# Hybrid attention encoder layer on one Trainium2 core: last down product in one group of nine feature pairs, sum over heads as two adds

## The chip, the cores and the metric

The kernel runs on one core of one Trainium2 chip. The metric is device time in microseconds (us); the figure for a kernel is the median of its runs. All tensors are float32. A matmul operand is split into a rounded high part and a remainder, and a product is made of three matmuls: high by high, high by remainder and remainder by high.

## The reference, cut to what matters

One encoder layer over 2048 tokens of width 1024. Half of the heads attend to all tokens, half to a window; each half is normalised over its 512 columns, and the two go through one output projection. A gated feed-forward block with 2816 features follows.

```python
def rms_norm(x, g):
    y = x * lax.rsqrt(jnp.mean(x * x, axis=-1, keepdims=True) + EPS)
    return y * g

mixed = jnp.concatenate([rms_norm(out_a, group_norm_a), rms_norm(out_b, group_norm_b)], -1) @ w_out
x = x + rms_norm(mixed, norm_mix_post)
h = rms_norm(x, norm_ffn_pre)
f = (jax.nn.silu(h @ w_gate) * (h @ w_up)) @ w_down
x = x + rms_norm(f, norm_ffn_post)
```

## The kernel before, in words

The program runs in stages: input projection and windowed attention (to about 590 us), the global attention with the output projection woven in (to about 1230 us), a short passage to the feed-forward part, the gate and up products, and the down products, which end the program. TensorE is PE below, VectorE DVE, ScalarE ACT, GpSimd POOL, and SP the engine that issues the DMAs.

**The planner.** Nearly all instructions are first recorded and then ordered by a planner (class `Plan`, from line 257). It has a cost for each instruction and latencies between engines, orders the whole program up to four times and keeps the pass that it finds shortest. Each engine executes its own queue strictly in the planned order, so an instruction that waits holds up all that stand behind it on its engine. As every instruction is issued from one place, the profile gives line 523 for all of them, and the rows are told apart by their tiles. A second copy of the program for large scores stands behind a branch and isn't executed.

**The sum over heads.** `out_half` (line 1418) handles one half (512 columns, 4 groups of 128) of one of the 16 token tiles, so it is called 32 times. It splits the half into `oh` and `ol`, squares it on ACT into the tile `sqo` (one buffer), and adds the four groups on DVE into `rd`, 128 x 128, at line 1445. A tiny matmul with `ones` sums `rd` further, and from this the scale `rg` of the half is made, with which the projected half leaves the PSUM.

```python
sq = op.tile([P, 512], F32, tag="sqo", bufs=1, name="sqo")
nc.scalar.activation(sq, o, AF.Square)
rd = op.tile([P, P], F32, tag="rd", bufs=1, name="rd")
nc.vector.tensor_reduce(rd, sq.rearrange("p (h c) -> p c h", h=4), axis=AX.X, op=ALU.add)
```

**The down products.** The feed-forward matrices are multiplied by a scheme of seven products of sums of quarters instead of eight. Each down product `p` is done for two halves `c` of the tokens. It adds over 11 feature pairs `j` (`NJ`) into four accumulators, one for each of four token tiles. For a pair it needs the activation side (`a_combo`, line 1683: a 256 KB load into `ar`, `ah` on ACT, `al` on DVE; four slots of each) and the weight side (`wd_combo`: `wdh` and `wdl`, 16 slots of each, 13 in one pool and 3 in another; a weight is kept for both values of `c`). `down_product` (line 1693) goes through the pairs in groups; within a group it takes accumulator by accumulator. Groups are single pairs, except in the very last call (`p` = 2, `c` = 1), whose last group has `TAIL` = 3 pairs.

**The end.** After the last product each of its four token tiles is finished (`finish`, line 1769): DVE adds the accumulator to a running total (tile `C`), ACT squares it (`junkf`) with a running sum, DVE multiplies by the gain (`gfp`) and adds the sums of squares (`fs`), POOL takes the power -1/2 (`fr`), and DVE, or for the second half of a row ACT and POOL, scale and add the residual (`st`), which SP writes out. For the last tile both halves are done on DVE. The residual rows are loaded into `st`, from `X`; of these buffers there are four.

Of the kernel before, what the change touches and what calls it, by code (L numbers as in the profile page):

```python
# [11 lines left out]
F32R = mybir.dt.float32r  # L12
AF = mybir.ActivationFunctionType
ALU = mybir.AluOpType
AX = mybir.AxisListType
# [3 lines left out]
P = 128  # L19
# [7 lines left out]
CH = 512  # L27
# [42 lines left out]
W_BUFS = 4  # L70
WD_L = 13
WD_R = 3
TAIL = 3
B_DVE = 13
B_DVE_U = (0, 2)
T_HI = 1
# [9 lines left out]
def f32(ap):  # L86
    return ap.bitcast(F32)
# [438 lines left out]
class Layer:  # L526
# [107 lines left out]
    def bank(self, pool, tag, bufs=1):  # L634
        return pool.tile([P, 512], F32, tag=tag, bufs=bufs, name=tag)
# [782 lines left out]
    def out_half(self, t, j, bank=None):  # L1418

        nc, op, sm = self.nc, self.op, self.sm  # L1420
        bank = bank or (lambda: self.bank(self.ps_a, "ow"))
        if j:
            o = op.tile([P, 512], F32, tag="ob", bufs=1, name="ob")
            self.load(o, self.OB[t])
            self.mixed[t] = op.tile([P, D], F32, tag="mix", bufs=1, name="mix")
        else:
            o = self.fin.pop(t)
        mix_ = self.mixed[t]
        h_ = op.tile([P, 512], F32R, tag="oh", name="oh")
        l_ = op.tile([P, 512], F32R, tag="ol", name="ol")  # L1430
        w = P if t == NT - 1 and j == 0 else 512
        for c in range(0, 512, w):
            self.urgent(LAST_UP if w == P else 0.0)
            nc.vector.tensor_copy(h_[:, c:c + w], o[:, c:c + w])
            self.urgent(0.0)
            yield GAP
            self.urgent(LAST_UP if w == P else 0.0)
            nc.vector.tensor_tensor(l_[:, c:c + w], o[:, c:c + w], f32(h_[:, c:c + w]), op=ALU.subtract)
            self.urgent(0.0)
            yield GAP  # L1440
        sq = op.tile([P, 512], F32, tag="sqo", bufs=1, name="sqo")
        nc.scalar.activation(sq, o, AF.Square)
        yield GAP
        rd = op.tile([P, P], F32, tag="rd", bufs=1, name="rd")
        nc.vector.tensor_reduce(rd, sq.rearrange("p (h c) -> p c h", h=4), axis=AX.X, op=ALU.add)
        rg = sm.tile([P, 1], F32, tag="rg", name="rg")

        def norm():
            self.urgent(HALF_UP if t == NT - 1 else 0.0)
            gs = bank()  # L1450
            nc.tensor.matmul(gs[:, 0:2], lhsT=rd, rhs=self.ones2, start=True, stop=True)
            self.rsqrt(rg, gs[:, 0:1], 512, 1)
            self.urgent(0.0)

        late = w == P
        if not late:
            norm()
            yield 430
        acc = [bank() for n in range(2)] if late else []
        for n in range(2):  # L1460
            cs = slice(n * 512, (n + 1) * 512)
            ps = acc[n] if late else bank()
            for p in range(4):
                pc = slice(p * P, (p + 1) * P)
                k = 4 * j + p
                nc.tensor.matmul(ps, lhsT=h_[:, pc], rhs=self.wo[2 * n][:, k], start=(p == 0), stop=False)
                yield 216
                nc.tensor.matmul(ps, lhsT=h_[:, pc], rhs=self.wo[2 * n + 1][:, k], start=False, stop=False)
                yield 216
                nc.tensor.matmul(ps, lhsT=l_[:, pc], rhs=self.wo[2 * n][:, k], start=False, stop=(p == 3))  # L1470
                yield 216
            if late and n == 0:
                norm()
            yield GAP2
            self.urgent(HALF_UP if t == NT - 1 else 0.0)
            if j:
                nc.scalar.activation(mix_[:, cs], ps, AF.Copy, scale=rg)
            else:
                nc.vector.scalar_tensor_tensor(mix_[:, cs], ps, rg, mix_[:, cs], op0=ALU.mult, op1=ALU.add)
            self.urgent(0.0)  # L1480
            yield GAP
        if not j:
            self.load(self.MX[t], self.mixed.pop(t))
# [174 lines left out]
    def wd_combo(self, p, j):  # L1658

        nc, fd = self.nc, self.fd  # L1660
        if p in self.B_SRC:
            src = self.wd_quarter(j, *self.B_SRC[p])
        elif p == 5:
            src = self.T[j] = self.fr.tile([P, CH], F32, tag=f"T{j}", bufs=1, name=f"T{j}")
            nc.gpsimd.tensor_tensor(src, self.wd_quarter(j, 0, 1), self.wd_quarter(j, 0, 0), op=ALU.subtract)
        elif p == 6:
            src = self.T[j]
            nc.gpsimd.tensor_tensor(src, self.wd_quarter(j, 1, 1), src, op=ALU.subtract)
        elif p == 4:
            src = self.T[j]  # L1670
            nc.gpsimd.tensor_tensor(src, src, self.wd_quarter(j, 1, 0), op=ALU.subtract)
        else:
            src, b = self.wd_quarter(j, 1, 1), self.wd_quarter(j, 0, 1)
            nc.gpsimd.tensor_tensor(src, src, b, op=ALU.subtract)
        pool, n = (fd, WD_L) if self.nwd % (WD_L + WD_R) < WD_L else (self.fr, WD_R)
        self.nwd += 1
        wh = pool.tile([P, CH], F32R, tag="wdh", bufs=n, name="wdh")
        wl = pool.tile([P, CH], F32R, tag="wdl", bufs=n, name="wdl")
        nc.scalar.activation(wh, src, AF.Copy)
        nc.vector.tensor_tensor(wl, src, f32(wh), op=ALU.subtract)  # L1680
        return wh, wl

    def a_combo(self, p, c, j):
        nc, fd = self.nc, self.fd
        st = fd.tile([P, CH], F32, tag="ar", bufs=3, name="ar")
        self.load(st, self.AC[c][j][:, p - 1])
        ah = fd.tile([P, CH], F32R, tag="ah", bufs=4, name="ah")
        al = fd.tile([P, CH], F32R, tag="al", bufs=4, name="al")
        nc.scalar.activation(ah, st, AF.Copy)
        nc.vector.tensor_tensor(al, st, f32(ah), op=ALU.subtract)  # L1690
        return ah, al

    def down_product(self, p, c, W, last=False):
        nc = self.nc
        acc = [self.gu_bank() for _ in range(4)]
        ends = list(range(1, self.NJ - TAIL + 1)) + [self.NJ] if last else range(1, self.NJ + 1)
        j0 = 0
        for j1 in ends:
            ops = []
            for j in range(j0, j1):  # L1700
                if (p, j) not in W:
                    W[p, j] = self.wd_combo(p, j)
                ops.append((j, *self.a_combo(p, c, j), *W[p, j]))
            for i in range(4):
                ts = slice(i * P, (i + 1) * P)
                for j, ah, al, wh, wl in ops:
                    nc.tensor.matmul(acc[i], lhsT=ah[:, ts], rhs=wh, start=(j == 0), stop=False)
                    nc.tensor.matmul(acc[i], lhsT=ah[:, ts], rhs=wl, start=False, stop=False)
                    nc.tensor.matmul(acc[i], lhsT=al[:, ts], rhs=wh, start=False, stop=(j == self.NJ - 1))
            j0 = j1  # L1710
        return acc
# [121 lines left out]
```

## Time and profile before

| | |
|---|---|
| median of 3 runs | 2554.9 us (2551.17 to 2563.43) |
| the profiled execution | 2557.14 us, its span 2555.3 us |
| busy in the span: PE, PE weight load | 2462.4 us (96%), 1945.0 us (76%) |
| busy in the span: DVE, ACT, POOL | 1877.8 us (73%), 1393.1 us (55%), 1473.4 us (58%) |

The span runs from the first to the last instruction in the profile; the rest of the execution's time lies around it. A row of a group shows its instructions' busy time, count and mean duration, then the idle time of its engine just before them and what ended it. A row of the timeline shows start, duration, engine and instruction; several alike in a row stand as x2, x3, with the time from the first start to the last end.

### The profile page before, as it was taken

The numbers are of one execution on the slowest core, as the hardware profiler recorded it, in microseconds if no ns is written. First come the engines' busy times: TensorE is split into PE (matmuls) and PEld (weight loads), VectorE is DVE, ScalarE is ACT, GpSimd is POOL, SyncE is SP. The second block draws the span as 40 slices with busy tenths as digits, with TensorE's granted clock in tenths as the row PEclk, the third lists the DMA queues.
The fourth block names the chain that finished last, engine by engine and source line by source line (L and its number), as shares of the span: only waits on it lengthen the run. The fifth ranks groups of instructions, "written<-read, shape, count | busy, mean of one in ns | idle before, by whom it ended". The sixth has DMA issues, their size and how long they took to land.

```text
span 2555.3 us, 34171 instructions
## 1 busy us (share of the span) xinstructions
PE 2462.4 (96%) x10604; PEld 1945.0 (76%) x10604; DVE 1877.8 (73%) x2864; ACT 1393.1 (55%) x2610; POOL 1473.4 (58%) x1175
## 2 busy tenths in 40 slices
PE   8999999899999999999899999999999999999997
PEld 6766677577877777777688888878888887888886
DVE  6777677789898988888877667796655556556755
ACT  5666566598888888878433333343332334433433
POOL 4333343379998889999365666755445443331333
PEclk9999999999999999999999999999999999999999
DMA  6555544443121313222544445563233227554664
GB/s 200 153 157 158 159 146 129 144 157 100 61 88 64 100 63 107 96 91 92 173 147 142 159 154 166 179 223 112 91 97 122 87 83 262 174 182 148 184 200 154
DMA packets 200896, 351.67 MB, mean 138 GB/s; under 512 B 26624, under 2 KB 82304, under 8 KB 200192
## 3 DMA queue, kind: packets, MB, share of 16 engines
q1 hardware_dynamic: 200704, 349.40, 42.5%
q8 instruction: 85, 1.39, 0.2%
q14 instruction: 107, 0.88, 0.1%
HBM read 229.85 MB, written 106.56 MB: 132 GB/s over the span
## 4 chain that ended last, share of the span: by engine, by line
PE 75%; DVE 7%; ACT 6%; DMA 5%; issue 4%; POOL 2%; SPq 1%; ACTq 0%; DVEq 0%; POOLq 0%
PE gu L523 31%; PE gv L523 18%; PE mm L523 6%; PE ow L523 6%; PE o L523 6%; PE a L523 4%; PE pp L523 3%; DVE pla L523 1%; DMA xn<-in_x_dram 1%; SPq L523 1%; ACT pha L523 1%; ACT mm L523 1%; POOL acc L523 1%; ACT nat L523 1%; DMA RB<-HL 1%
## 5 line engine op out<-in xcount | busy, mean ns | idle before, releaser
L523 POOL TENSOR_TENSOR acc<-acc,pha 128x512 f32<-128x512 f32 x408 | 561.3, 1386 | 48.9 <-ACT pha L523 22.5
L523 POOL TENSOR_TENSOR s<-wraw 128x512 f32<-128x512 f32 x88 | 124.3, 1425 | 304.4 <-DMA wraw<-in_w_up_dram 179.5
L523 PE MATMUL gu<-xl,wh 128*128 128x512 f32 x776 | 294.1, 396 | 0.0
L523 PE MATMUL gu<-xh,wl 128*128 128x512 f32 x776 | 288.1, 397 | 4.2 <-DVE wl L523 4.1
L523 PE MATMUL gu<-xh,wh 128*128 128x512 f32 x776 | 288.2, 397 | 1.8 <-ACT wh L523 1.8
L523 DVE TENSOR_TENSOR pla<-mm,pha 128x512 fp32r<-128x512 f32 x370 | 246.3, 682 | 34.4 <-ACT pha L523 24.0
L523 ACT ACTIVATE wh<-s 128x512 fp32r<-128x512 f32 x176 | 110.8, 630 | 281.5 <-PE gu L523 160.4
L523 PE MATMUL mm<-R,kt 128*128 128x512 f32 x740 | 251.0, 400 | 6.0 <-DVE pla L523 4.9
L523 PE MATMUL pp<-w_in,xh 128*128 128x512 f32 x720 | 239.2, 404 | 16.5 <-ACT w_in L523 10.9
L523 POOL TENSOR_TENSOR c<-c,c 128x512 f32<-128x512 f32 x132 | 203.4, 1557 | 77.5 <-DVE c L523 52.3
L523 DVE TENSOR_TENSOR al<-ar,ah 128x512 fp32r<-128x512 f32 x154 | 140.1, 913 | 146.9 <-ACT ah L523 131.7
L523 ACT ACTIVATE mm<-mm 128x512 f32<-128x512 f32 x370 | 214.6, 591 | 28.5 <-PE mm L523 26.1
L523 ACT ACTIVATE ah<-ar 128x512 fp32r<-128x512 f32 x154 | 97.0, 630 | 224.7 <-PE gu L523 137.2
L523 DVE TENSOR_TENSOR c<-gu,c 128x512 f32<-128x512 f32 x174 | 116.4, 686 | 115.8 <-PE gu L523 115.3
L523 DVE TENSOR_TENSOR wl<-s,wh 128x512 fp32r<-128x512 f32 x176 | 164.9, 942 | 20.9 <-ACT wh L523 11.5
L523 PE MATMUL gv<-xl,wh 128*128 128x512 f32 x456 | 175.1, 396 | 2.2 <-DVE xl L523 2.2
L523 PEld LDWEIGHTS gu<-xh,wl 128*128 128x128 f32 x776 | 146.1, 189 | 39.2 <-DVE wl L523 5.0
L523 ACT ACTIVATE wh<-wraw 128x512 fp32r<-128x512 f32 x132 | 83.0, 628 | 168.3 <-PE gu L523 97.6
L523 PEld LDWEIGHTS gu<-xh,wh 128*128 128x128 f32 x776 | 146.3, 189 | 36.9 <-ACT wh L523 2.7
L523 PEld LDWEIGHTS mm<-R,kt 128*128 128x128 f32 x740 | 134.7, 188 | 50.2 <-DVE pla L523 21.2
L523 PEld LDWEIGHTS pp<-w_in,xh 128*128 128x128 f32 x720 | 136.0, 191 | 48.5 <-ACT w_in L523 13.1
L523 PEld LDWEIGHTS gu<-xl,wh 128*128 128x128 f32 x776 | 146.4, 189 | 34.5
(257 smaller groups left out, 6522.0 us busy)
## 6 DMA issues: line engine op xcount, KB each, us to landing
AC<-c SPq DMA_DIRECT2D x154, 256.0 KB
ar<-AC SPq DMA_DIRECT2D x154, 256.0 KB
wdr<-in_w_down_dram SPq DMA_DIRECT2D x99, 256.0 KB
wraw<-in_w_gate_dram SPq DMA_DIRECT2D x20, 1024.0 KB
wraw<-in_w_up_dram SPq DMA_DIRECT2D x20, 1024.0 KB
R<-QA SPq DMA_DIRECT2D x128, 128.0 KB
st<-XB SPq DMA_DIRECT2D x40, 256.0 KB
xn<-in_x_dram SPq DMA_DIRECT2D x16, 512.0 KB
```

Of the source, the lines that this page charges most:

```text
L523: op.call(*[real(a) for a in op.args], **{k: real(v) for k, v in op.kw.items()})
```

## The change

Two edits. `TAIL` goes from 3 to 9, so the last call's groups are pair 0, pair 1, and then pairs 2 to 10 together. Nine pairs need nine slots for the activation side at once, where there are four; the activation sides of pairs 2 to 6 go into weight slots of which five are free by then (16 less the 11 weights of that product), through the new argument `spare`. In the planned order these five read `wdh<-ar` and `wdl<-ar`. In `out_half` the reduction becomes two additions, 128 x 256 in place in `sqo` and 128 x 128 into `rd`.

```diff
-TAIL = 3
+TAIL = 9
...
-        nc.vector.tensor_reduce(rd, sq.rearrange("p (h c) -> p c h", h=4), axis=AX.X, op=ALU.add)
+        nc.vector.tensor_tensor(sq[:, 0:2 * P], sq[:, 0:2 * P], sq[:, 2 * P:4 * P], op=ALU.add)
+        nc.vector.tensor_tensor(rd, sq[:, 0:P], sq[:, P:2 * P], op=ALU.add)
...
+        wh, wl = self.wd_tiles()
...
-    def a_combo(self, p, c, j):
+    def wd_tiles(self):
+        pool, n = (self.fd, WD_L) if self.nwd % (WD_L + WD_R) < WD_L else (self.fr, WD_R)
+        self.nwd += 1
+        return [pool.tile([P, CH], F32R, tag=tag, bufs=n, name=tag) for tag in ("wdh", "wdl")]
+
+    def a_combo(self, p, c, j, spare=False):
         nc, fd = self.nc, self.fd
         st = fd.tile([P, CH], F32, tag="ar", bufs=3, name="ar")
         self.load(st, self.AC[c][j][:, p - 1])
-        ah = fd.tile([P, CH], F32R, tag="ah", bufs=4, name="ah")
-        al = fd.tile([P, CH], F32R, tag="al", bufs=4, name="al")
+        if spare:
+            ah, al = self.wd_tiles()
+        else:
+            ah = fd.tile([P, CH], F32R, tag="ah", bufs=4, name="ah")
+            al = fd.tile([P, CH], F32R, tag="al", bufs=4, name="al")
...
-                ops.append((j, *self.a_combo(p, c, j), *W[p, j]))
+                ops.append((j, *self.a_combo(p, c, j, last and j < j1 - 4 and j >= self.NJ - TAIL), *W[p, j]))
```

Since the planner orders the program as a whole, its order differs from the first use of `rd` on, about 590 us into the program, and not only where instructions were exchanged.

The end of DVE's queue, the work on the last token tiles (`C` a running total, `fs` a sum of squares, `st` an output row). Before:

```order
L523 TENSOR_TENSOR C_21369<-gu,C_21369 128x512
L523 SCALAR_TENSOR_TENSOR fs_24439<-fsq 128x1
L523 TENSOR_TENSOR C_21369<-C_21369,gfp 128x512
L523 SCALAR_TENSOR_TENSOR fs_24451<-fsq 128x1
L523 TENSOR_TENSOR C_21369<-C_21369,gfp 128x512
L523 TENSOR_TENSOR C_21369<-gu,C_21369 128x512
L523 SCALAR_TENSOR_TENSOR st<-C_21369,fr,st 128x512
L523 TENSOR_TENSOR C_21369<-C_21369,gfp 128x512
L523 SCALAR_TENSOR_TENSOR fs_24465<-fsq 128x1
L523 SCALAR_TENSOR_TENSOR st<-C_21369,fr,st 128x512
L523 SCALAR_TENSOR_TENSOR st<-C_22428,fr,st 128x512
L523 SCALAR_TENSOR_TENSOR st<-C_21369,fr,st 128x512
```

and now:

```order
L523 SCALAR_TENSOR_TENSOR fs_24449<-fsq 128x1
L523 TENSOR_TENSOR C_21384<-C_21384,gfp 128x512
L523 SCALAR_TENSOR_TENSOR st<-C_21384,fr,st 128x512
L523 TENSOR_TENSOR C_21384<-gu,C_21384 128x512
L523 SCALAR_TENSOR_TENSOR fs_24483<-fsq 128x1
L523 TENSOR_TENSOR C_21384<-C_21384,gfp 128x512
L523 SCALAR_TENSOR_TENSOR st<-C_21384,fr,st 128x512
L523 TENSOR_TENSOR C_21384<-gu,C_21384 128x512
L523 TENSOR_TENSOR C_21384<-C_21384,gfp 128x512
L523 SCALAR_TENSOR_TENSOR fs_24501<-fsq 128x1
L523 SCALAR_TENSOR_TENSOR st<-C_22475,fr,st 128x512
L523 SCALAR_TENSOR_TENSOR st<-C_21384,fr,st 128x512
```

Before, the steps of the last three tiles are mixed; now each tile goes from its addition to its output row before the next begins.

SP's queue over the last product: activation loads (`ar` from `AC`, the digit is the pair), residual rows (`st` from `X`) and outputs. Before:

```order
L523 DMA out_dram<-st 128x512
L523 DMA ar<-AC_8_224 128x512
L523 DMA out_dram<-st 128x512
L523 DMA st<-X_181 128x1024
L523 DMA out_dram<-st 128x512
L523 DMA ar<-AC_9_225 128x512
L523 DMA out_dram<-st 128x512 x2
L523 DMA ar<-AC_10_226 128x512
L523 DMA out_dram<-st 128x512 x2
```

and now:

```order
L523 DMA ar<-AC_7_223 128x512
L523 DMA ar<-AC_8_224 128x512
L523 DMA out_dram<-st 128x512 x2
L523 DMA ar<-AC_9_225 128x512
L523 DMA out_dram<-st 128x512
L523 DMA st<-X_181 128x1024
L523 DMA ar<-AC_10_226 128x512
L523 DMA out_dram<-st 128x512 x3
```

The loads of pairs 7 and 8 moved ahead of all outputs, and that of pair 10 from behind the sixth output to behind the third.

DVE's queue at the first of the 32 sums over heads (`pla` the remainders of the attention weights). Before:

```order
L523 TENSOR_TENSOR oa<-o_6138,oa 64x512
L523 TENSOR_REDUCE rd<-sqo 128x128
L523 TENSOR_TENSOR pla<-a_6444,pha 128x512
L523 TENSOR_SCALAR ms<-ow 128x1
L523 TENSOR_TENSOR pla<-mm,pha 128x512
```

and now:

```order
L523 TENSOR_TENSOR sqo<-sqo 128x256
L523 TENSOR_TENSOR pla<-mm,pha 128x512
L523 TENSOR_TENSOR oa<-a_6295,oa 64x512
L523 TENSOR_TENSOR pla<-mm,pha 128x512
L523 CAST pha<-mm 128x512
L523 RECIPROCAL cmpa<-cmpa 16x64
L523 TENSOR_TENSOR pla<-mm,pha 128x512
L523 TENSOR_TENSOR pla<-a_6503,pha 128x512
L523 TENSOR_TENSOR pla<-mm,pha 128x512 x2
L523 CAST pha<-mm 128x512
L523 TENSOR_TENSOR pla<-mm,pha 128x512
L523 TENSOR_TENSOR rd<-sqo 128x128
```

The two additions don't stand together: the second is 12 instructions behind the first.

## Rows read from the trace of the kernel before

**Rows 1.** The page: busy time, share of the span and instructions of each engine.

```profile
PE 2462.4 (96%) x10604; PEld 1945.0 (76%) x10604; DVE 1877.8 (73%) x2864; ACT 1393.1 (55%) x2610; POOL 1473.4 (58%) x1175
```

**Rows 2.** Windows: stretch, length, busy PE, PEld, DVE, ACT, POOL; PE clock, DMA, GB/s.

```profile
590.00:1230.00 640.00, 622.90 (x2676) 486.35 (x2676) 562.46 (x842) 518.41 (x964) 577.87 (x447) 1.00 0.25 83
1230.00:1260.00 30.00, 23.01 (x83) 17.42 (x84) 26.09 (x40) 12.36 (x23) 12.48 (x9) 0.89 0.57 187
1260.00:2540.00 1280.00, 1274.00 (x5545) 1035.68 (x5544) 846.64 (x1063) 473.09 (x821) 616.15 (x425) 1.00 0.48 155
2540.00:2556.00 16.00, 2.10 (x10) 1.40 (x8) 8.65 (x13) 3.79 (x9) 7.32 (x6) 0.72 0.37 137
```

**Rows 3.** PE's waits from 590 to 1260 us: total, times, longest.

```profile
PE mm L523 <- DVE pla L523: 3.7, 10, 0.8
...
PE ow L523 <- DVE rd L523: 0.5, 1, 0.5
```

**Rows 4.** End of the chain of waits (start, length, what): last matmuls, last DVE work.

```profile
2511.95 28.57 PE gu L523 x126
...
2549.27 0.44 DVE st L523
```

**Rows 5.** DVE's timeline over the end: the first tile, then the last.

```profile
2536.70 0.69 DVE L523 TENSOR_TENSOR C<-gu,C 128x512 f32<-128x512 f32 x1 [2.50 <-PE gu L523]
2538.24 0.69 DVE L523 TENSOR_TENSOR C<-C,gfp 128x512 f32<-128x512 f32 x1 [0.85 <-ACT junkf L523]
2538.85 0.15 DVE L523 SCALAR_TENSOR_TENSOR fs<-fsq 128x1 f32<-128x1 f32 x1
...
2539.73 0.75 DVE L523 SCALAR_TENSOR_TENSOR st<-C,fr,st 128x512 f32<-128x512 f32 x1
...
2543.05 0.68 DVE L523 TENSOR_TENSOR C<-gu,C 128x512 f32<-128x512 f32 x1
...
2548.30 1.41 DVE L523 SCALAR_TENSOR_TENSOR st<-C,fr,st 128x512 f32<-128x512 f32 x2 [0.44 <-POOL fr L523]
```

**Rows 6.** POOL's timeline: the first tile's power.

```profile
2539.15 0.55 POOL L523 TENSOR_TENSOR fr<-fs,mhalf 128x1 f32<-128x1 f32 x1 [8.31 <-DVE fs L523]
```

**Rows 7.** SP's timeline over the last product: a residual row, the last activation load.

```profile
2521.65 0.38 SPq L523 DMA_DIRECT2D st<-X  x1
...
2529.72 0.33 SPq L523 DMA_DIRECT2D ar<-AC  x1
```

**Rows 8.** ACT's timeline: the last pair's rounding.

```profile
2532.84 0.63 ACT L523 ACTIVATE ah<-ar 128x512 fp32r<-128x512 f32 x1 [3.19 <-DMA ar<-AC]
```

**Rows 9.** DVE's timeline over the last product: first total, last remainders.

```profile
2511.08 1.37 DVE L523 TENSOR_TENSOR C<-gv,C 128x512 f32<-128x512 f32 x2 [0.46 <-PE gv L523]
...
2527.92 4.07 DVE L523 TENSOR_TENSOR al<-ar,ah 128x512 fp32r<-128x512 f32 x3
2533.51 0.69 DVE L523 TENSOR_TENSOR al<-ar,ah 128x512 fp32r<-128x512 f32 x1 [1.52 <-ACT ah L523]
```

**Rows 10.** The tiles `rd`, `ol` and `acc`: count, shortest, median, longest in ns, starts.

```profile
L523 DVE TENSOR_REDUCE rd<-sqo x32: 1027/1076/1097, 588.8 to 1236.6; 128x128 f32<-128x512 f32 x32
...
L523 DVE TENSOR_TENSOR ol<-oa,oh x19: 275/677/1485, 616.5 to 1236.4; 128x512 fp32r<-128x512 f32 x15, 128x128 fp32r<-128x128 f32 x4
L523 DVE TENSOR_TENSOR ol<-ob,oh x16: 674/916/1671, 604.0 to 1217.3; 128x512 fp32r<-128x512 f32 x16
...
L523 POOL TENSOR_TENSOR acc<-acc,pha x357: 1265/1298/2677, 589.5 to 1219.2; 128x512 f32<-128x512 f32 x179
```

**Rows 11.** DVE groups by shape: count, busy us, mean ns.

```profile
L523 DVE TENSOR_REDUCE rd<-sqo 128x128 f32<-128x512 f32 x32 | 34.3, 1073 | 0.3 <-ACT sqo L523 0.2
...
L523 DVE TENSOR_TENSOR ol<-ob,oh 128x512 fp32r<-128x512 f32 x16 | 16.1, 1007 | 0.1
```

**Rows 12.** The chain, 560 to 1250 us: reductions of 0.9 us or more on it.

```profile
588.82 1.05 DVE rd L523
...
1011.17 1.01 DVE rd L523
```

More of the change, by code (lines that the diff above doesn't have):

```diff
@@ L1674, in wd_combo @@
             nc.gpsimd.tensor_tensor(src, src, b, op=ALU.subtract)
[L1675 to L1678, printed above, removed]
+        wh, wl = self.wd_tiles()
         nc.scalar.activation(wh, src, AF.Copy)
```

## The prediction, made before the changed kernel was run

> **What bounds the kernel now.** I read the page first, then the windows by stage, then the chain of waits at its end, and last the timelines and tiles that the change touches. PE is busy 96% of the span [rows 1], so whatever doesn't take idle time away from PE, or work away from behind its last matmul, is worth nothing. The windows say where such time is [rows 2]: 640 - 622.9 = 17.1 us of PE idle in the global attention, 30 - 23.0 = 7.0 us in the passage behind it, 1280 - 1274.0 = 6.0 us in all of the feed-forward part up to 2540 us, and then a tail in which PE has nothing left to do. In the attention PE mostly waits for DVE, in many short pieces; the sum over heads is named once, with 0.5 us [rows 3]. The tail is read from the end of the chain [rows 4]: the last matmul ends at 2511.95 + 28.57 = 2540.52 us, the last DVE instruction at 2549.27 + 0.44 = 2549.71 us. These 9.19 us are the only place where the first edit can gain.
>
> **Edit 1, what it takes from the tail.** Take one tile with nobody ahead of it. The first tile's addition starts at 2536.70, its square follows on ACT, then the gain's product at 2538.24, the sum of squares at 2538.85 [rows 5], the power on POOL at 2539.15 [rows 6], and its first output row runs from 2539.73 to 2540.48 [rows 5]: 3.78 us in all. The last tile has two such rows on DVE, which take 1.41 us instead of 0.75, so it would need 4.44 us. It took more: its addition began only at 2543.05, 2.53 us behind the last matmul, because three other tiles were still in DVE's queue, and it ended 6.66 us later [rows 5].
>
> The four accumulators end, counted in the planned order of matmuls, 24, 15, 7 and 0 matmuls before the last one; now 45, 33, 12 and 0. One matmul is 28.57 / 126 = 0.227 us [rows 4]. The third tile therefore starts 12 x 0.227 = 2.7 us before the end, and in the new DVE order its output row stands ahead of the fourth tile's addition. It is through at -2.7 + 3.8 = +1.1 us, and the fourth ends at 1.1 + 4.4 = 5.5 us, against 9.2. That is 3.7 us. The ends: 4.8 us if the fourth tile starts at once (9.2 - 4.4), 1.4 us if its own chain stays as long as it was (9.2 - 1.1 - 6.7). I take 3.5, near the unqueued first tile, since the new order removes the queue. What follows the last row (its DMA, the end of the program) is the same in both.
>
> **Edit 1, what it costs ahead of the tail.** The first accumulator now has to end 45 x 0.227 = 10.2 us before the last matmul, at about 2530.3, and needs the last pair by then. Before, that pair's load was issued at 2529.72 [rows 7], rounded on ACT at 2532.84 [rows 8] and its remainder made at 2533.51 to 2534.20 [rows 9]. All of this must come some 4 us earlier. The load: it now stands right behind the residual row X_181, which was issued at 2521.65 [rows 7]; with the 3.1 us that it took from issue to rounding it is there at about 2525, and the load is no problem. DVE is: from 2511.08 to 2534.20 it was idle little more than the 1.52 us in the row, and three remainders took 4.07 us, 1.36 each where the last took 0.69 [rows 9]. In the new order seven remainders stand behind the first of these additions, where there were eight; the previous accumulators end about 7 matmuls (1.6 us) earlier. So the last remainder comes at 2534.2 - 1.5 - 1.4 - 1.6 = 2529.7 us, 0.6 us before it is needed. A late one costs PE its lateness. I put 1 us here, between 0 and 4 (the whole advance that is asked for). The work itself is unchanged: as many loads, splits and matmuls as before; only the place of five pairs differs.
>
> Edit 1 together: 3.5 - 1.0 = 2.5 us gained, between 4.8 and a loss of 2.6 (1.4 - 4).
>
> **Edit 2, the sums over heads.** Removed are 32 reductions of 1.073 us, 34.3 us of DVE [rows 11]. Added are 32 pairs. The trace shows no such pair; the nearest is the remainder `ol`, which like them reads two tiles in SBUF: at its shortest 0.275 us for 128 columns and 0.674 us for 512 [rows 10], so by the straight line 0.41 us for 256. A pair is then 0.41 + 0.28 = 0.69 us at the least, 21.9 us in all. But the same rows show waiting: the `ob` form takes 1.007 us in the mean [rows 11], 0.33 above its shortest, and up to 1.671, while the reductions stay within 1.027 and 1.097 [rows 10]. If each of the two waits 0.33, a pair costs 1.35 us and all 43.2. DVE's work changes by -12.4 to +8.9 us. Little of that reaches PE. DVE is busy 562 of 640 us [rows 2], and only four of the 32 reductions stand on the chain with about 1 us each [rows 12]; 4 x 0.38 = 1.5 us gained or 4 x 0.28 = 1.1 lost. The second addition is 12 instructions behind the first at the first sum, so the scale `rg` comes later, but PE waited 0.5 us for `rd` in all [rows 3], and the out-projection that uses it is spread over a tile's 40 us. I take 0.
>
> The Trainium skill has a rule that speaks against this edit ("SBUF — State Buffer", section "Who interferes with whom"): a VectorE instruction with two SBUF inputs contends with a GpSimd instruction that reads SBUF, whichever starts first blocking the other, while a tensor_reduce never contends on this chip. By that rule, the trace agrees: the remainders spread from 0.674 to 1.671 us and the reductions by 7%; the sum by the rule is the 43.2 us end, that without it the 21.9 us end.
>
> **The moved order.** From the first sum on, the planner's order is another one. What this does can't be read from the trace of before. It can at most give back the idle time of PE from 590 to 2540 us, 17.1 + 7.0 + 6.0 = 30 us; nothing excludes a loss. I take 0, with a third of the attention's and passage's 24 us, 8 us, to either side.
>
> **The sum.** The profiled execution took 2557.1 us, 2.2 above the median. 2557.1 - 2.5 = 2554.6, and against the median 2554.9 - 2.5 = 2552.4; I say **2552 us**. A measurement of this kernel can tell some 0.5%, 12.8 us, from no change, so this is "the same".
>
> **Rivals.**
> - The last pair is late. DVE doesn't keep up behind 2511 us, PE waits in the last product for as long as the tail gains, and the time stays at 2555. For it: the 1.36 us remainders and only 0.6 us to spare. Against: three of the five spare-slot remainders are made ahead of the crowded stretch. Chance 0.15.
> - POOL becomes the bound of the attention; slower. POOL is busy 577.9 of 640 us, more than DVE [rows 2], and its additions into `acc`, 1.298 us in the median, stretch to 2.677 [rows 10], as the remainders on DVE do. If each pair keeps it from its tiles for 0.69 us, 22 us come on top, 600 of 640. It decides if POOL's remaining idle time lies where its work isn't there yet, so that it can't catch up: then the stage grows by up to 22 us, to 2574. Against it: the sums come once in 20 us, and POOL's 62 us of idle time are three times the addition. The Trainium skill's rule above is the one from which this follows. Chance 0.05.
> - The new order meets PE's idle time better, and 12 of the 24 us in the attention and the passage go: 2540. For it: DVE is released earlier at 32 places. Against: no row says which of the waits goes. Chance 0.1. The contrary, an order that costs 12 us or more, 0.03, at 2565.
> - The change doesn't do what it says, if the nine pairs found no slots early enough and were split one by one as before; the new SP order, with pair 8 ahead of all outputs, speaks against it. This would be 2555 and is held in the first rival.
>
> **How the numbers follow.** The forecast has 1 - 0.15 - 0.05 - 0.1 - 0.03 = 0.67. Its own range is 2554.9 - 4.8 - 1.5 - 8 = 2541 to 2554.9 + 2.6 + 1.1 + 8 = 2567, with all ends at once, which is unlikely; the range that holds 8 in 10 leaves out the POOL case, the costly order and the last of these ends: 2541 to 2562. Faster by over 0.5% is the case of the better order and a little of the forecast's edge, 0.11; slower by over 0.5% are POOL and the costly order, 0.08; the rest, 0.81, is within 0.5%.
>
> **What would show it.** Right: from the last matmul to the last DVE instruction 5 to 6.5 us instead of 9.2, the fourth addition within 1.5 us of the last matmul, and no PE wait over 1 us in the last 30 us; `sqo` and `rd` additions with a spread like that of `ol`, 0.7 to 1.35 us for a pair; PE's idle time from 590 to 1260 us within 8 us of 24. Wrong: a PE wait for `al` or `wdl` near 2530 us (first rival), POOL over 97% busy in the attention with PE waiting behind it (second), or a change of the attention stage of over 10 us in either direction, which would make the tail a side matter.

## The result, and the profile after

The changed kernel takes 2580.44 us (median of 7 runs, 2573.89 to 2593.14) against 2557.37 us (7 runs, 2551.17 to 2566.26) on the same chip: **ratio 1.0097, 95% interval 1.0072 to 1.0122**. It is slower by about 1%, outside the predicted range of 2541 to 2562 us. The profiled execution took 2580.44 us, its span is 2578.6 us.

The page after, busy time by engine, answers to [rows 1]:

```profile
PE 2468.4 (96%) x10604; PEld 1946.3 (75%) x10604; DVE 1895.8 (74%) x2896; ACT 1392.6 (54%) x2610; POOL 1475.5 (57%) x1175
```

PE has the same 10604 matmuls and 6 us more busy time, DVE 32 instructions and 18.0 us more. That doesn't make 23 us. The stages do. The global attention ends where the first matmul of the gate and up products (`gu<-xh,wh`) starts. PE's timeline has it before:

```profile
1231.61 0.50 PE L523 MATMUL gu<-xh,wh 128*128 128x512 f32 x1
```

and after:

```profile
1260.72 0.50 PE L523 MATMUL gu<-xh,wh 128*128 128x512 f32 x1 [0.38 <-ACT wh L523]
```

Up to 590 us the two agree within 2 us, so nearly all of the 29.1 us arise in this stage. Its windows (columns as in [rows 2]), before and then after:

```profile
590.00:1231.61 641.61, 624.10 (x2681) 487.03 (x2681) 564.07 (x845) 519.93 (x966) 578.45 (x448) 1.00 0.25 84
```

```profile
590.00:1260.72 670.72, 631.99 (x2685) 489.81 (x2683) 592.37 (x879) 521.01 (x969) 578.28 (x449) 0.99 0.25 80
```

PE is busy 7.9 us longer with the same matmuls and idle 38.7 us instead of 17.5: 7.9 + 21.2 = 29.1. DVE has 28.3 us more work in it, nearly the stage's growth. POOL has none (578.45 and 578.28). The waits of PE in this stage after, answering to [rows 3] (total, times, longest):

```profile
PE mm L523 <- DVE pla L523: 12.2, 16, 1.9
PE o L523 <- DVE ala L523: 5.5, 4, 2.8
PE a L523 <- DVE pla L523: 4.5, 5, 2.1
...
PE a L523 <- DVE oa L523: 3.4, 1, 3.4
```

PE waits for DVE as before, but longer: 12.2 us in 16 waits on the first line, where it was 3.7 in 10 [rows 3]. And the work on DVE itself, the additions by shape (count, busy us, mean ns), then their shortest, median and longest:

```profile
L523 DVE TENSOR_TENSOR sqo<-sqo 128x256 f32<-128x256 f32 x32 | 29.7, 927 | 0.1
...
L523 DVE TENSOR_TENSOR rd<-sqo 128x128 f32<-128x128 f32 x32 | 23.0, 718 | 0.1
...
L523 DVE TENSOR_TENSOR oa<-oa,dena 128x512 f32<-128x512 f32 x15 | 18.7, 1248 | 1.5 <-DMA dena<-RDA 1.4
```

```profile
L523 DVE TENSOR_TENSOR sqo<-sqo x32: 409/913/1514, 591.0 to 1263.6; 128x256 f32<-128x256 f32 x32
```

A pair takes 0.927 + 0.718 = 1.645 us, not the 0.69 to 1.35 us of the prediction, and 52.7 us in all against the reductions' 34.3 [rows 11]. The other 10 of DVE's 28 us are mostly old instructions that also read two SBUF tiles and became longer: `oa<-oa,dena` had 905 ns before, and `ol<-ob,oh` went from 1007 [rows 11] to 1145.

**The rest of the program.** From the first gate product to the last matmul it took 1310.5 us before and 1306.4 after. The last matmul, before and after, in PE's timeline:

```profile
2541.71 0.39 PE L523 MATMUL gu<-wdh,al 128*128 128x512 f32 x1
```

```profile
2566.74 0.39 PE L523 MATMUL gu<-wdh,al 128*128 128x512 f32 x1
```

DVE's timeline at the end after, answering to the last of [rows 5]:

```profile
2564.44 0.69 DVE L523 TENSOR_TENSOR C<-gu,C 128x512 f32<-128x512 f32 x1 [0.66 <-PE gu L523]
...
2567.19 0.75 DVE L523 SCALAR_TENSOR_TENSOR st<-C,fr,st 128x512 f32<-128x512 f32 x1 [0.44 <-POOL fr L523]
2567.86 0.68 DVE L523 TENSOR_TENSOR C<-gu,C 128x512 f32<-128x512 f32 x1
...
2570.88 1.41 DVE L523 SCALAR_TENSOR_TENSOR st<-C,fr,st 128x512 f32<-128x512 f32 x2 [0.73 <-POOL fr L523]
```

Last matmul to last DVE instruction: 2549.71 - 2542.10 = 7.6 us before, 2572.29 - 2567.13 = 5.2 us after, 2.4 less. The account of the span is 29.1 (attention) - 4.1 (feed-forward) - 2.4 (tail) + 0.7 (behind it) = 23.3 us, the difference of the spans. A difference of 4 us in the feed-forward part is no finding: among kernels with the same order there it lay between 1302.8 and 1310.7 us (table below).

### The profile page after: what moved, and what is told of

Its sections match the earlier page's. It is cut to its first block, busy times and chain, and to the rows that moved or that the text cites. A ratio compares the mean times of both kernels' runs of the same rounds, so it can differ in the third digit from the quotient of the medians.

```text
span 2578.6 us, 34155 instructions
## 1 busy us (share of the span) xinstructions
PE 2468.4 (96%) x10604; PEld 1946.3 (75%) x10604; DVE 1895.8 (74%) x2896; ACT 1392.6 (54%) x2610; POOL 1475.5 (57%) x1175
## 4 chain that ended last, share of the span: by engine, by line
PE 70%; DVE 10%; DMA 6%; ACT 5%; issue 4%; POOL 3%; SPq 1%; ACTq 0%; DVEq 0%; POOLq 0%
PE gu L523 29%; PE gv L523 17%; PE mm L523 6%; PE o L523 6%; PE ow L523 5%; PE pp L523 3%; PE a L523 3%; DVE pla L523 2%; POOL acc L523 2%; SPq L523 1%; DVE st L523 1%; ACT pha L523 1%; DMA xn<-in_x_dram 1%; DMA wraw<-in_w_in_dram 1%; DMA out_dram<-st 1%
## 5 line engine op out<-in xcount | busy, mean ns | idle before, releaser
L523 PE MATMUL pp<-w_in,xh 128*128 128x512 f32 x720 | 238.1, 403 | 17.5 <-ACT w_in L523 10.7
L523 DVE TENSOR_TENSOR al<-ar,ah 128x512 fp32r<-128x512 f32 x149 | 134.1, 905 | 137.4 <-ACT ah L523 108.0
L523 DVE TENSOR_TENSOR wl<-s,wh 128x512 fp32r<-128x512 f32 x176 | 170.3, 972 | 21.2 <-ACT wh L523 10.7
L523 PE MATMUL ow<-wo,oh 128*128 128x512 f32 x488 | 166.9, 399 | 5.9 <-DVE mix L523 3.4
```

What stands on the lines that cost most here:

```text
L523: op.call(*[real(a) for a in op.args], **{k: real(v) for k, v in op.kw.items()})
```

## Experiments

All runs in one table. "Stage" is from 590 us to the first gate product, "DVE" its busy time in it, "ff" from there to the last matmul, "tail" from there to the last DVE instruction; all in us, of the profiled execution. The medians of before in the five groups of runs were 2554.9 to 2556.8. A stage is read from one execution: in the four kernels that keep the order and whose ratio can't be told from 1 it is 639.9 to 641.6 us.

| run | median (runs) | ratio to before, 95% | stage | DVE | ff | tail |
|---|---|---|---|---|---|---|
| before | | | 641.6 | 564.1 | 1310.5 | 7.6 |
| the change | 2580.4 (7) | 1.0097, 1.0072–1.0122 | 670.7 | 592.4 | 1306.4 | 5.2 |
| tail9_old_order | 2552.5 (10) | 0.9990, 0.9978–1.0003 | 641.5 | 562.2 | 1307.3 | 5.2 |
| sums_only | 2580.9 (4) | 1.0097, 1.0073–1.0122 | 671.1 | 591.7 | 1302.6 | 7.6 |
| adds_in_old_order | 2568.5 (7) | 1.0052, 1.0033–1.0071 | 657.3 | 577.4 | 1306.2 | 7.6 |
| reduce_in_new_order | 2572.7 (7) | 1.0064, 1.0043–1.0084 | 662.0 | 575.4 | 1305.9 | 7.6 |
| padded_reduce | 2565.8 (10) | 1.0040, 1.0027–1.0052 | 654.2 | 578.6 | 1310.0 | 7.6 |
| half_padded | 2561.3 (7) | 1.0035, 1.0020–1.0051 | 650.5 | 573.1 | 1307.6 | 7.6 |
| pad_behind | 2566.4 (5) | 1.0045, 1.0026–1.0064 | 655.5 | 580.3 | 1304.0 | 7.6 |
| two_halves | 2557.0 (10) | 1.0011, 0.9997–1.0026 | 639.9 | 564.0 | 1310.7 | 7.6 |
| short_reduce | 2555.8 (10) | 1.0002, 0.9986–1.0017 | 640.9 | 543.0 | 1302.8 | 7.6 |
| order_cost538 | 2568.6 (7) | 1.0047, 1.0030–1.0064 | 649.6 | 569.5 | 1316.2 | 7.6 |
| order_cost1073 | 2557.0 (10) | 1.0005, 0.9990–1.0020 | 653.5 | 582.2 | 1298.2 | 7.6 |
| true_costs | 2595.4 (4) | 1.0158, 1.0139–1.0177 | 670.9 | 585.0 | 1320.2 | 5.3 |
| tail9_own_order | 2567.4 (5) | 1.0051, 1.0034–1.0069 | 650.0 | 574.1 | 1314.1 | 5.3 |
| tail9_cost1073 | 2554.2 (10) | 0.9988, 0.9975–1.0002 | 655.6 | 577.9 | 1298.0 | 5.2 |

**The two edits apart.** The nine pairs alone, with the attention's order kept as before (the planner is made to take its third pass, as it did for before):

```diff
-TAIL = 3
+TAIL = 9
...
-            if best is None or self.makespan < best:
+            if best is None or i == 2:
```

> Only the last down product is changed (TAIL = 9 with the spare slots); the sum over heads stays one reduction, and the planner is held to its third pass, so that the attention stage keeps the order that it has before. Theory A (the loss sits in the attention stage and comes from the two adds or from the order that they bring): about 4 us faster than before, some 2553, with 5 to 6 us from the last matmul to the last DVE instruction. Theory B (the larger last group itself costs PE time in the feed-forward part): slower than before by more than 5 us.

The sums alone, with `TAIL` at 3 and the two additions of the change in `out_half`:

```diff
-        nc.vector.tensor_reduce(rd, sq.rearrange("p (h c) -> p c h", h=4), axis=AX.X, op=ALU.add)
+        nc.vector.tensor_tensor(sq[:, 0:2 * P], sq[:, 0:2 * P], sq[:, 2 * P:4 * P], op=ALU.add)
+        nc.vector.tensor_tensor(rd, sq[:, 0:P], sq[:, P:2 * P], op=ALU.add)
```

> Only the two adds, TAIL = 3; its order up to the first gate product is nearly that of the changed kernel (11 of 4939 PE rows stand elsewhere). Theory A: slower than before by 25 to 29 us, that is the whole loss of the change plus the 4 us of the tail. Theory B: no more than 5 us slower.

The sums carry the whole loss: the same ratio as the change and a stage of 671.1 us. Theory A holds: 1.0097 is 24.8 us, against its 25 to 29. The nine pairs leave the stage alone and shorten the tail by 2.4 us; at 0.9990 with an interval that holds 1 they are worth at most 6 us and perhaps nothing, where theory A had 4.

**The additions and the order apart.** The planner orders with one reduction as before, and where it stands two additions are issued back to back:

```diff
+            self.plan.record("DVE", "tensor_reduce", adds, (rd, sq), {})
```

> The two adds are executed, one right behind the other, at the place where the reduction stands before; the planner still plans with the one reduction, so that every other instruction keeps its place. Theory A1 (the adds themselves cost the time, because they wait for POOL and hold it up): the pair takes 1.3 to 1.7 us instead of 1.07 and the kernel is slower than before by 10 us or more. Theory A2 (the order costs the time): within 5 us of before.

The other half: ordered as if there were two additions, but the first is not issued and the reduction is issued in the second's place:

```diff
+            self.plan.record("DVE", "tensor_tensor", lambda *args, **kw: None,
+                             (sq[:, 0:2 * P], sq[:, 0:2 * P], sq[:, 2 * P:4 * P]), dict(op=ALU.add))
+            self.plan.record("DVE", "tensor_tensor", lambda r, *args, **kw: V.tensor_reduce(
+                r, sq.real().rearrange("p (h c) -> p c h", h=4), axis=AX.X, op=ALU.add),
+                             (rd, sq[:, 0:P], sq[:, P:2 * P]), dict(op=ALU.add))
```

> The reverse: the planner plans with the two adds, but the first is not issued and the reduction is executed in place of the second, so that every other instruction stands as with the two adds alone (TAIL = 3). Theory A1: within 5 us of before, since no add waits for POOL. Theory A2: as slow as the two adds alone, 20 us or more above before.

Both cost, so neither A1 nor A2 is the whole. The additions in the old order add 15.7 us to the stage, the new order with the old reductions 20.4; together they would make 36, the change has 29.1, so they overlap by a fifth. Even in the old order a pair takes 1.585 us:

```profile
L1447 DVE TENSOR_TENSOR sqo<-sqo 128x256 f32<-128x256 f32 x32 | 29.7, 928 | 0.6 <-ACT sqo L523 0.6
...
L1448 DVE TENSOR_TENSOR rd<-sqo 128x128 f32<-128x128 f32 x32 | 21.0, 657 | 1.1
```

**Is it DVE's time, or something else in the additions?** The old order and the old reduction, with a second reduction ahead of it that reads one SBUF tile, nothing but time on DVE (its result is overwritten):

```diff
+            V.tensor_reduce(r[:, 0:1], s[:, 0:432], axis=AX.X, op=ALU.add)
             V.tensor_reduce(r, s.rearrange("p (h c) -> p c h", h=4), axis=AX.X, op=ALU.add)
```

> Old order, TAIL = 3. The reduction stays, and right ahead of it DVE executes a second, useless reduction over 432 columns of the squares (one input in SBUF), about 0.55 us, so that the pair takes DVE some 1.6 us, as the two adds did, but holds POOL nowhere. The useless sum is overwritten. Theory C1 (DVE's time itself is what PE waits for): the attention stage grows by 13 to 18 us, as with the two adds in the old order (15.7). Theory C2 (what costs is that adds and POOL hold each other up): less than 6 us.

And less time, a quarter of the sum:

```diff
+            V.tensor_reduce(r, s[:, 0:P].rearrange("p (h c) -> p c h", h=1), axis=AX.X, op=ALU.add)
```

> Old order, TAIL = 3. The reduction takes only the first of the four groups of 128 columns (the other three are left out of the sum), some 0.3 us instead of 1.07. Theory C1: DVE's time is on the path, and PE's idle time in the attention stage shrinks, by 5 to 17 us. Theory C3 (the old order leaves slack for what is planned, and only what comes late costs): less than 4 us faster.

The window of the padded run, and then of the short one, over their stages:

```profile
590.00:1244.18 654.18, 629.49 (x2680) 486.85 (x2681) 578.64 (x875) 520.43 (x965) 575.50 (x448) 0.99 0.25 82
```

```profile
590.00:1230.89 640.89, 624.64 (x2688) 488.29 (x2687) 543.00 (x848) 521.81 (x970) 581.39 (x450) 1.00 0.25 84
```

DVE has 14.6 us more in the padded run, and the stage 12.6, a little under C1's 13 to 18; C2 falls. In the short run, whose kernel leaves out three quarters of the sum, DVE has 21.1 us less, and the stage 0.7: here C1 falls and C3 holds. Time added on DVE reaches PE for the most part; time taken away from the same places gives nothing. So most of what the additions cost in the old order is their length.

Half the padding shows whether there is slack that the first part of it would use up:

```diff
-            V.tensor_reduce(r[:, 0:1], s[:, 0:432], axis=AX.X, op=ALU.add)
+            V.tensor_reduce(r[:, 0:1], s[:, 0:144], axis=AX.X, op=ALU.add)
```

> As the padded run, every instruction planned and placed as before, but the extra reduction ahead of each sum over heads sums 144 columns instead of 432: about 0.29 us more of DVE per sum (from 0.275 us for 128 columns and 0.592 us for 432), 9.3 us in all, where the padded run added 18.9 us and lost 12.6 us in the stage and 10 in the time. F1, DVE's queue has no slack at the sums, each added time passes on: half the padded run's loss, stage 6 us longer (about 648), ratio about 1.002. F2, DVE has slack of some tenths of a us at the sums, and only what exceeds it is lost: stage within 2 us of 641.6, ratio below 1.001.

There is none: 9.1 us more of DVE, 8.9 us more stage. That was more than F1 had for it, and half the padding cost over two thirds of the whole. Two causes other than time could do that: that a second instruction stands there at all, or that the sum `rd`, behind the extra instruction, is late. The same time as two instructions, each a reduction of half of the columns:

```diff
+            for c in (0, 64):
+                V.tensor_reduce(r[:, c:c + 64], s.rearrange("p (h c) -> p c h", h=4)[:, c:c + 64], axis=AX.X, op=ALU.add)
```

> Everything planned and placed as before, but each reduction of 512 columns into 128 is issued as two reductions of 256 columns into 64 each, with the same sums; together about as long as the one (by the line through 0.275 us for 128 columns and 1.073 for 512, 0.54 us each, 1.08 to 1.15 a pair). F1, time in DVE's queue is what costs: 0 to 2 us of the stage, ratio below 1.0015. F3, a second instruction at that place costs by itself: about 9 us of the stage, as with the half padding, ratio about 1.0035.

And the padding behind the sum instead of ahead of it:

```diff
             V.tensor_reduce(r, s.rearrange("p (h c) -> p c h", h=4), axis=AX.X, op=ALU.add)
+            V.tensor_reduce(s[:, 0:1], s[:, 80:512], axis=AX.X, op=ALU.add)
```

> Planned and placed as before; the extra reduction of 432 columns (0.59 us, its result, one column of the squares, is used by nobody) stands behind the real one instead of ahead of it, so that the sum itself is as early as before and only what follows in DVE's queue is late. F1, the queue behind is what costs: about the padded run's loss, stage 10 to 13 us longer, ratio about 1.004. F4, the late sum costs, through the scale that waits for it: stage within 3 us of 641.6, ratio below 1.0015.

The rows of the two halves and their window, then the window with the padding behind:

```profile
L1448 DVE TENSOR_REDUCE rd<-sqo 128x64 f32<-128x256 f32 x64 | 36.3, 607 | 0.3 <-ACT sqo L523 0.2
```

```profile
590.00:1229.87 639.87, 622.94 (x2676) 485.56 (x2674) 564.03 (x872) 517.87 (x963) 577.21 (x446) 1.00 0.26 84
```

```profile
590.00:1245.49 655.49, 631.15 (x2687) 487.91 (x2686) 580.27 (x879) 523.64 (x970) 580.38 (x450) 0.99 0.25 82
```

A second instruction without more time costs nothing (stage 1.7 us shorter, DVE's time equal). Padding behind the sum costs as much as ahead of it (13.9 us, DVE 16.2 more). So it is the queue: what stands behind the sums on DVE comes later, and PE waits for that. F1 holds in kind, F2, F3 and F4 fall. Of the 9.1, 14.6 and 16.2 us added, 8.9, 12.6 and 13.9 us show in the stage; by the ratios it is 8.9, 10.2 and 11.5 us, so between 0.7 and 1 of what was added.

**Is the new order bad because the planner has wrong prices?** It plans the reduction at 603 ns and the two additions at 336 + 202 = 538 ns. The reduction kept and planned at 538, and at the 1073 that it takes:

```diff
             n = free_size(args[1])
+            if n == 512 and free_size(out) == 128:
+                return 538.0
```

> The computation of before, TAIL = 3, one reduction; only the planner's cost of that reduction is 538 ns instead of 603 (the sum of what it plans for the two adds). This moves PE's order from the first sum on. Theory D1 (almost any other order than the one the constants were chosen under loses): 8 to 20 us slower than before. Theory D2 (the loss of the new order comes from the two adds standing apart): within 5 us of before.

> As the run with 538 ns, but with the 1073 ns that the trace shows for the reduction as the planner's cost. Theory D1: 8 to 20 us slower than before. Theory D2: within 5 us of before, or faster, since the plan is nearer to what happens.

The same kernel, only ordered otherwise: 12 us lost with one price, as D1 had it, and nothing with the other, as D2 had it. With 1073 the stage is 11.9 us longer and the feed-forward part 12.3 us shorter; work of the second has moved into the first, so the stage alone isn't a measure where the order changes. With 538 both are longer. The change itself with the durations that its trace shows as prices:

```diff
+        if eng == "DVE" and method == "tensor_tensor" and out.root.name in ("sqo", "rd"):
+            return 927.0 if n == 256 else 718.0
```

> The changed kernel (nine pairs, two additions), but the planner is told what the two additions took on the chip in it, 927 and 718 ns instead of 336 and 202. E1, the order went wrong because the additions were planned too cheap: with their price known the planner fills DVE's queue otherwise, the order's 16 us go and the additions' 13 us stay; stage from 590 us to the first gate product about 655 to 658 us, time 2557 + 13 - 4 = 2566 us. E2, the order of before was simply a favourable one and any new order loses some of that: stage 660 to 672 us, time 2570 to 2582 us.

The nine pairs with the reduction at 1073, and at its old price with the pass that the planner then prefers:

> Nine pairs and the reduction, planned at the 1073 ns that it takes. If the tail's 4 us are independent of what comes before, they come on top of the run with this planned cost and three pairs (2557.0 against a before of 2556.8): 2553 us, ratio 0.998 to 0.999. If the new order is yet another draw in the attention, anything from 2548 to 2569 us; the stage's length tells which.

> Nine pairs and the reduction at its old planned cost, the order being the one that the planner itself then chooses (another of its passes than for before, so that the attention's order differs as a whole). E1, orders planned with the same wrong price are about alike: stage within 5 us of 641.6 and time about 2553 us. E2, each new order is a draw that costs 0 to 16 us against that of before: stage 642 to 662 us, time 2553 to 2569 us, or lower if the order of before was not the best.

True prices made it worse, 2595.4 us: E1 falls, and E2 had 2582 as its upper end for that run. E2 holds as far as it says that a new order is a draw: orders planned with the reduction cost 0 to 13 us, those planned with the additions 16 (above) or more. The nine pairs' shorter tail is there in all five kernels that have them. By the medians it comes on top of the order at 1073 (2554.2 us, where three pairs had 2557.0), but the intervals of the two ratios overlap. What in these orders costs time is not settled. In reduce_in_new_order DVE has 11.3 us more in the stage with the same instructions, in the ones with two SBUF inputs: `oa<-oa,dena` 1195 ns against 905, `ol<-oa,oh` 1070 against 830. So such instructions meet POOL's more often there; whether that causes the loss or only goes with it, no run tells; order_cost1073, which costs nothing, has them longer too (1101 and 1028 ns). Two more things stand out in reduce_in_new_order: in the stage POOL waits 36.0 us for the work behind the sums (`rg` for DVE's `ms`, 11.8 before), and the trace has PE's granted clock at the lower of its two levels for 20.5 us (3.4 before). Neither is what makes an order dear in general: tail9_own_order costs 13 us with 11.8 and 3.4. That true_costs costs 15 us more than the change is unexplained too; 14 of them lie in ff.

No run beats before by more than can be told: 2552.5 and 2554.2 us, for the nine pairs with the reduction, both have 1 within their intervals.

## Why the prediction was wrong, point by point

**The tail: right in kind, the gain 2.4 us instead of 3.5.** The forecast from the last matmul to the end was 5.5 us, it measured 5.2, and the fourth addition began 0.73 us behind the last matmul. What failed is the starting point of 9.19 us. The piece of the chain in [rows 4] ends at the last matmul *on the chain*, which is the third accumulator's; the fourth one's last matmul ended 7 matmuls later, at 2542.10, and the tail before was 7.6 us. Both were at hand: the 7 matmuls are in the prediction's own count of the accumulators' ends, and [rows 2] has PE busy for 2.10 us behind 2540 us. The fourth addition before thus began 0.95 us behind the last matmul, not 2.53. A chain leaves an engine where another takes over, not where that engine ends.

**The last pair: no wait there.** The last product begins at 2536.7 us, and PE waits nowhere in it, so the 1 us that was put down (0 to 4) was 0. Waits that the kernel before doesn't have stand earlier, two products ahead, in PE's timeline after:

```profile
2480.66 0.50 PE L523 MATMUL gu<-wdh,ah 128*128 128x512 f32 x1 [1.21 <-ACT ah L523]
...
2488.14 0.50 PE L523 MATMUL gu<-wdh,al 128*128 128x512 f32 x1 [0.66 <-DVE al L523]
```

They make 1.9 us. They are not the last pair's, and what brings them is not shown: of the other kernels with nine pairs, tail9_old_order and tail9_cost1073 have 1.7 and 2.0 us in that stretch, true_costs and tail9_own_order 0.2 and 0.1. With them the first edit nets 2.4 - 1.9 = 0.5 us in the changed kernel; without them 2.4, near the forecast 2.5, but by luck, since 3.5 and 1.0 were both too large.

**The sums over heads: the step that failed first.** The upper bound of a pair, 1.35 us, gave each addition the mean wait of `ol`, 0.33 us. They waited 0.927 - 0.409 = 0.52 and 0.718 - 0.272 = 0.45 us over their shortest, so a pair was 1.645. The shortest two make 0.681 us, as the line through `ol` had it (0.69): the uncontended price was right, the wait was not a constant to be carried from one instruction to another. The Trainium skill's rule ("SBUF — State Buffer", section "Who interferes with whom"), a VectorE instruction with two SBUF inputs contends with a GpSimd instruction that reads SBUF and a tensor_reduce doesn't, agrees with the trace: the reductions of halves stayed near 607 ns and those of the padding at 592, while the first of the additions spread from 409 to 1514.

All 64 additions after bear it out. Of the 32 first ones, the 8 that began with no POOL instruction running took 410 to 427 ns; of the other 24, 22 ended 278 to 286 ns behind the end of POOL's instruction, however long that still ran. Of the second ones, 7 began so and took 274 to 283 ns; of the other 25, 23 ended 118 to 181 ns behind POOL's. Of the 32 reductions before, 25 also began while POOL ran, and all stayed within 1.027 and 1.097 us [rows 10]. So the wait is what is left of POOL's instruction. An addition ahead of POOL's, and then a place where they meet:

```profile
798.58 0.28 DVE L523 TENSOR_TENSOR rd<-sqo 128x128 f32<-128x128 f32 x1
798.74 0.55 POOL L523 TENSOR_TENSOR rg<-ms,mhalf 128x1 f32<-128x1 f32 x1 [1.15 <-DVE ms L523]
```

```profile
1151.79 1.30 POOL L523 TENSOR_TENSOR acc<-acc,pha 128x512 f32<-128x512 f32 x1
...
1152.19 1.05 DVE L523 TENSOR_TENSOR rd<-sqo 128x128 f32<-128x128 f32 x1
...
1153.16 1.78 DVE L523 TENSOR_TENSOR ol<-oa,oh 128x512 fp32r<-128x512 f32 x1
...
1154.86 1.75 DVE L523 TENSOR_TENSOR ala<-acc,aha 128x512 fp32r<-128x512 f32 x1
...
1156.03 1.71 POOL L523 TENSOR_TENSOR st<-st 128x512 f32<-128x512 f32 x1
...
1156.54 1.48 DVE L523 TENSOR_TENSOR sqo<-sqo 128x256 f32<-128x256 f32 x1
...
1157.94 0.67 DVE L523 TENSOR_TENSOR oa<-a,oa 64x512 f32<-64x512 f32 x1
1158.67 0.79 PE L523 MATMUL a<-pla,vt 128*128 128x512 f32 x1 [3.42 <-DVE oa L523]
```

There `rd` begins while POOL works and ends 0.15 us behind POOL's end at 1153.09, and `sqo`, of the next sum, 0.28 us behind POOL's at 1157.74. The next DVE instruction stands behind it, and PE, which needs that, waits 3.42 us. The additions are only a part of this wait: `sqo` took 1.07 us over its shortest, and between the two stand `ol` and `ala`, old instructions with two SBUF inputs, which also met POOL's.

**"Little of that reaches PE": the step that failed for the additions.** It was argued from four of 32 reductions on the chain [rows 12] and DVE's 78 us of idle time [rows 2]. The first says what taking time away can bring, and there it was right (short_reduce: 0.7 us of 21, and a time that can't be told from before). It says nothing of time added. DVE's idle time isn't slack either, since an in-order queue that waits for ACT or PE can't use it for what comes later: with the old order 9.1 us added on DVE cost the stage 8.9, 14.6 cost 12.6 and the additions' 13.3 cost 15.7 (13.3 by their ratio). By a rate of about one, the prediction's own upper end of +8.9 us would have given 2552.4 + 8.9 = 2561, the edge of its range, and the measured pairs 2571.

**The moved order: the step that failed for the rest.** It was put at 0 with 8 us to either side and 0.03 for one that costs 12 us. Alone it costs 16 (1.0064, interval 1.0043 to 1.0084), where the additions alone cost 13 (1.0052, 1.0033 to 1.0071): the term put at 0 was worth at least about as much as the additions. Other orders cost 0 to 13, and what makes one dear stays open. None of the six other orders that ran beat the one of before by more than can be told: in these the draw wasn't symmetric.

**The rivals.** POOL as the bound falls: its busy time in the stage is the same to 0.2 us, and its `acc` additions took 1393 ns before and 1396 after. The contention was there, but in the sum DVE paid for it. What POOL does show is the scales coming late: its idle time for `rg` behind DVE's `ms`, before, then after:

```profile
POOL rg L523 <- DVE ms L523: 11.8, 7, 6.4
```

```profile
POOL rg L523 <- DVE ms L523: 41.1, 20, 7.3
```

The late last pair and the better order didn't come, and the nine pairs found their slots (the trace after has five `wdl<-ar`). The costly order was right and had too small a chance. The sign of "a change of the attention stage of over 10 us would make the tail a side matter" was the one that came.

## What to carry to other kernels

On an in-order engine that another one waits for often, price an added instruction at its full length (0.7 to 1 of it reached PE here), and a removed one at what the chain of waits has of it: the two aren't the same rate. Where an engine at 90% shares SBUF with the one that gets the new instruction, look for a form with one SBUF input before one with fewer elements; a reduction of 1.07 us was cheaper than two additions whose shortest sum to 0.68. And when an edit makes a scheduler reorder a tuned program, hold the order still in one run and the edit still in another before you believe either.

## What was not expected of the hardware

A wait of PE can cost more than its length, since the granted clock behind it can be lower. After the wait of 3.42 us above, the windows of 10 us on both sides have a granted clock of 1.00, 0.89 and 0.77, and two shorter ones show the two levels, 1.2 GHz (0.50) and 2.4 GHz (1.00):

```profile
1140.00:1150.00 10.00, 8.98 (x42) 6.82 (x41) 8.73 (x12) 7.94 (x16) 8.94 (x7) 1.00 0.00 1
1150.00:1160.00 10.00, 6.48 (x26) 5.00 (x25) 8.30 (x10) 4.75 (x9) 7.98 (x7) 0.89 0.25 80
1160.00:1170.00 10.00, 10.00 (x37) 8.00 (x37) 5.34 (x11) 4.00 (x7) 3.57 (x4) 0.77 0.24 95
...
1158.00:1164.00 6.00, 5.33 (x13) 4.17 (x14) 3.82 (x7) 0.59 (x1) 1.14 (x1) 0.50 0.19 75
1165.00:1170.00 5.00, 5.00 (x25) 4.14 (x24) 2.21 (x6) 3.33 (x6) 3.57 (x4) 1.00 0.22 84
```

The same two matmuls in them, at the lower and then at the higher level:

```profile
1159.69 1.05 PE L523 MATMUL ow<-wo,oh 128*128 128x512 f32 x2
...
1167.48 0.61 PE L523 MATMUL ow<-wo,oh 128*128 128x512 f32 x2
```

The trace has the lower level for 17.1 us of this stage after, beside waits of 1.9, 3.4 and 2.8 us (at 1054.8, 1158.7 and 1188.4 us), and for 3.4 us before. At half the speed the 13.7 us more are worth at most 6.8 of the 7.9 us by which PE's busy time grew over the stage; that is an estimate from these numbers. It isn't so for every wait: the waits of 2.1 us at 936.3 and 2.4 us at 1210.3 have no such stretch behind them. Nor is it the only way in which PE's busy time grows: in pad_behind it grew by 7 us with 6.8 us of the lower level, 3.4 more than before.
